# Shared expert's weights fetched early and used whole in float32 in the second mixture's first blocks

## Chip, cores and metric

One NeuronCore of a Trainium2 chip runs the whole kernel. The metric is the time of one execution in device microseconds, the median of three runs.

## What is computed

Two transformer blocks in a row on 1024 tokens of width 1024. Each is a mixer and a mixture of experts. The change lies at the seam inside the second block, between its mixer's last product and its mixture:

```python
mix = hybrid_mixer(h, ...)                      # ends with mix @ w_out
h = layer_norm(DEEPNORM_ALPHA * h + mix, ln1_g, ln1_b)
scores = jax.nn.sigmoid((xt @ w_router).astype(jnp.float32))
# top 4 of 8 groups, top 8 of 64 experts, tokens sorted by expert
yb = lax.map(block_ffn, (xin, blk_e))           # (silu(x @ w_gate[e]) * (x @ w_up[e])) @ w_down[e]
routed = jax.ops.segment_sum(y_assign, stok, num_segments=T)
shared = (jax.nn.silu(xt @ ws_gate) * (xt @ ws_up)) @ ws_down
h = layer_norm(DEEPNORM_ALPHA * h + routed + shared, ln2_g, ln2_b)
```

All inputs are float32. `ws_gate` and `ws_up` are 1024 x 256, `ws_down` is 256 x 1024: 3 MB, as each of the 64 routed experts.

## The kernel before

The program is written out by hand in the order in which each engine runs it. `mixer_out2` (line 2367) ends the second mixer: it loads `w_out` in eight pieces of 512 KB into staging places named `wo` (pool `pr`, six of them), splits every piece into a high and a low float32r part (`split`, line 240: a copy on ScalarE, a subtraction on VectorE), and then goes over the token tiles t of 128 rows: the product by `w_out` (L271 to L273, three float32r products in place of one float32 product), the layer norm (`norm`), the transposes and the router's logits of tile t - 2 (L2431, L2438). The normed rows go to `h2_d` in DRAM, scaled ones to the sum `acc_d`. The routing of tiles 0 to 3 is done in the middle (`route2`), that of tiles 4 to 7 later (`route_late`).

`moe2` (line 2569) makes a list of blocks: five token tiles for the shared expert (blocks 0 to 4), the 64 routed experts in some 100 blocks of up to 128 gathered rows (block 5 is the first), and the last three token tiles for the shared expert again. `experts` (line 1389) runs them. A block is: its rows into `xg` (`gather`), eight transposes (`trans`, L1584), the products by gate and up (`gate_up`), silu (`act`), two transposes (`h_trans`, L1643), the product by down (`down`), and an indirect DMA on GpSimd's queue that adds the result to `acc_d` (L1696).

Weights come in thirds of 1 MB (`wthird`: gate and up of half the rows twice, then down), each into one of `RAW2` = 11 places `raw` that are used in turn; third j waits until third j - 11 is freed. `pump` issues on SP's queue, in order, whatever has room; before the experts' order is known (`route` yields `ids`) it may issue only the first three thirds, those of the shared expert. An expert whose `whole` is true uses its places in float32 as they are (L1480); of another, `wsplit` writes float32r parts, in six pieces, into `gh`, `gl`, `dh`, `dl`, and the products are three float32r products each (L271 to L273). In the first blocks GpSimd makes some of the low parts (`LOD`). Routed experts that fit into 128 rows are whole, the others and the shared one are split.

While the shared blocks run, the table `ROUTE` says after which step of which block the next piece of the routing is issued: the rest of `route2`, then `rank` (the count of tokens for each expert, L2526, and the order of the experts, `ids`), the turned masks (L2551, L2559), and the tables of rows (`onehot`, `tabmm`, L1499, L1509), from which the first gathers of routed rows come. The five shared token tiles are loaded on SP's queue (L1572): tiles 0 to 3 right behind the shared weights, tile 4 after the routed thirds that `pump` has issued by then.

At the end `Last` takes places of the same ring (`room`) for the rows of `acc_d` and for the second norm's vectors.

Of the kernel before, what the change touches and what calls it, by code (L numbers as in the profile page):

```python
# [7 lines left out]
F32 = mybir.dt.float32  # L8
# [223 lines left out]
class Body:  # L232
# [1156 lines left out]
    def experts(self, cx, blocks, xsrc, wsrc, acc_d, C, route, pre=None, fin=None, whole=lambda key: False):  # L1389
# [4 lines left out]
        nc, tc = self.nc, self.tc  # L1394
        wp = cx.enter_context(tc.tile_pool(reuse_waits="tile", name="mw", bufs=2))
# [4 lines left out]
        n0 = next(n for n, b in enumerate(blocks) if b[0] is not None)  # L1400
# [10 lines left out]

        RAW = self.RAW1 if pre else self.RAW2
        raw, src, freed, ready, gone = dict(pre or {}), {}, [0], [not n0], set()
# [8 lines left out]
        def place(j):  # L1422
            if pre and j % RAW < 4:
                return self.big.tile([128, 2048], F32, name=f"b{3 - j % RAW}")
            return wp.tile([128, 2048], F32, name="raw", bufs=RAW - 4 if pre else RAW)

        def room():
            return wp.tile([128, 2048], F32, name="raw", bufs=RAW)

# [136 lines left out]
        def gather(n):  # L1566
            if n >= N:
                return
            r, t, _, R = blocks[n]
            xg = ep.tile([128, D], F32, name="xg", bufs=3)  # L1570
            if r is None:
                nc.sync.dma_start(xg, xsrc[t * 128:t * 128 + 128])  # L1572
            else:
                nc.gpsimd.indirect_dma_start(out=xg[:R], out_offset=None, in_=xsrc,
                                             in_offset=bass.IndirectOffsetOnAxis(ap=idx[n][0], axis=0))
            XG[n] = xg
# [134 lines left out]
        route = route(p1, ep)  # L1711
# [55 lines left out]
        for i, key in enumerate(keys[1:], 1):  # L1767
# [3 lines left out]
            if n0 and i > 2 and len(w) > 2:  # L1771
                w = w[1:]
# [189 lines left out]
    LOD = (0, 2, 5), (0, 3, 5)  # L1962
    LOD0 = (5,), (1, 3)

    def wthird(self, w, src, q):
# [402 lines left out]
    def mixer_out2(self, mo):  # L2368
# [5 lines left out]
        with ExitStack() as cx:  # L2374

            wr = cx.enter_context(tc.tile_pool(reuse_waits="tile", name="pr", bufs=1))
            wp = cx.enter_context(tc.tile_pool(reuse_waits="tile", name="pw", bufs=1))
# [8 lines left out]
            for n in range(4):  # L2386
                h = wp.tile([128, KT, 256], F32R, name="woh", bufs=4)
                lo = wp.tile([128, KT, 256], F32R, name="wol", bufs=4)
                for q in range(2):
                    w = wr.tile([128, 4, 256], F32, name="wo", bufs=6)  # L2390
                    nc.sync.dma_start(w, IN["w_out_2"][0][q * 512:q * 512 + 512, n * 256:n * 256 + 256]
                                      .rearrange("(k p) n -> p k n", p=128))
                    self.split(w, h[:, q * 4:q * 4 + 4], lo[:, q * 4:q * 4 + 4])
                W.append((h, lo))
# [39 lines left out]
            def router(t):  # L2434
# [8 lines left out]
                if t == 3:  # L2443
                    for _ in self.route2(rtp, lg[0], bias, 0, 4):
                        pass
            self.route_late = lambda rp: self.route2(rp, lg[1], bias, 4, 8)

            loadx(0)
            loadx(1)
            for t in range(10):  # L2450
                ts_ = slice(t * 128, t * 128 + 128)
                for half in range(2):
# [124 lines left out]
    def moe2(self, rt):  # L2577
# [28 lines left out]
        with ExitStack() as cx:  # L2606
            tp = cx.enter_context(tc.tile_pool(reuse_waits="tile", name="rt4", bufs=1))

            def route(p1, ep):
# [18 lines left out]
                for r in order:  # L2628
                    yield r
                    if r == "mask" and "pos" not in R:  # L2630
# [5 lines left out]
            fin = Last(self, cx, 8 - self.NT)  # L2636
            self.experts(cx, blocks, self.h2_d, wsrc, acc_d, C, route, fin=fin,
                         whole=lambda key: isinstance(key, int) and cap[key] <= C)

# [24 lines left out]
    def run(self):  # L2664
        tc, nc = self.tc, self.nc
        with ExitStack() as ctx:
# [49 lines left out]
            if "mxh" in self.dbg:  # L2716
                nc.sync.dma_start(self.dbg["mxh"].rearrange("k p s -> p k s"), self.mgh.bitcast(F32))
                nc.sync.dma_start(self.dbg["mxl"].rearrange("k p s -> p k s"), self.mgl.bitcast(F32))
            rp = rt.enter_context(tc.tile_pool(reuse_waits="tile", name="rt2", bufs=1))
            self.mixer_out2(rp)  # L2720
            u2.close()
# [32 lines left out]
```

## Time and profile before

| | |
|---|---|
| runs | 3248.46, 3254.14, 3257.79 us; median 3254.14 |
| profiled execution | 3251.11 us, its span 3249.3 us |
| PE, busy | 2940.6 us (90%) |
| VectorE, ScalarE, GpSimd busy | 1883.4 (58%), 1303.0 (40%), 924.9 us (28%) |
| mean granted TensorE clock | 0.952 |
| bytes read and written | 470.22 and 106.64 MB, 178 GB/s over the span |

`mixer_out2` runs from about 1981 to 2138 us, the five shared blocks from 2136 to 2256, the routed ones to about 3180, and the second norm to the end. PE stands for TensorE, DVE for VectorE, ACT for ScalarE, POOL for GpSimd, SP for the queue of SyncE that issues most DMAs. Times in rows are us from the span's start. A row of the timeline gives start, duration, engine, line, operation, tiles, shapes and count, and in brackets the idle time just before it and what ended it. The granted clock is a share of 2.4 GHz: 0.50 is the lower of the two levels, 1.2 GHz.

### The profile page before, as it was taken

Reading aid. Unit: us, or ns where it says so; the run is one execution under the profiler, and the core shown is the slowest. Engines: PE = TensorE matmul, PEld = TensorE weight load, DVE = VectorE, ACT = ScalarE, POOL = GpSimd, SP = SyncE. Lnnn points to the kernel's source line nnn. Section 1 sums busy time; section 2 is a strip of 40 time slices with the busy share of each in tenths; the row PEclk is TensorE's granted clock in tenths of the full one; section 3 lists DMA queues with packets and bytes.
Section 4 is the critical chain, followed back from the end, with each engine's and each line's share of the span. In section 5 each row is a group of like instructions: output and inputs, shape, how many; then the busy total and the mean of one; then the engine's idle time right before and its main releaser. Section 6 shows DMA issues by size and latency. Waiting matters only on the chain. (4 is left out here: it accounts for less than half of the span.)

```text
span 3249.3 us, 42976 instructions
## 1 busy us (share of the span) xinstructions
PE 2940.6 (90%) x16117; PEld 2229.6 (69%) x16117; DVE 1883.4 (58%) x2968; ACT 1303.0 (40%) x2000; POOL 924.9 (28%) x675
## 2 busy tenths in 40 slices
PE   5999999998988996999789998856999999999994
PEld 4778778886777894555479878845666666666553
DVE  5554651667777745655455566544655555555556
ACT  3332331445665423444343333332444444444442
POOL 0000000135777412333211132121333332323223
PEclk9999999998999997999899998968999999999997
DMA  3112120343223367999710003336989999999994
GB/s 113 65 52 85 65 88 7 121 158 93 86 89 92 102 240 251 309 336 350 245 53 27 27 17 101 107 116 224 289 273 320 323 317 314 313 310 317 315 287 140
DMA packets 225893, 579.79 MB, mean 178 GB/s; under 512 B 22421, under 2 KB 104005, under 8 KB 225653
## 3 DMA queue, kind: packets, MB, share of 16 engines
q1 hardware_dynamic: 188240, 445.42, 39.1%
q0 software_dynamic: 37008, 131.50, 16.3%
q8 instruction: 129, 2.11, 0.3%
q14 instruction: 84, 0.69, 0.1%
q10 hardware_dynamic: 432, 0.06, 0.0%
HBM read 470.22 MB, written 106.64 MB: 178 GB/s over the span
## 5 line engine op out<-in xcount | busy, mean ns | idle before, releaser
L1480 PE MATMUL gups<-raw,x 128*128 128x512 f32 (+1 forms) x680 | 299.2, 592 | 0.0
L271 PE MATMUL mm<-uh,wh 128*128 128x512 f32 x640 | 253.8, 396 | 10.8 <-ACT t L505 8.8
L273 PE MATMUL mm<-uh,wl 128*128 128x512 f32 x640 | 252.4, 394 | 0.0
L272 PE MATMUL mm<-ul,wh 128*128 128x512 f32 x640 | 251.7, 393 | 0.0
L1696 POOL DMA_INDIRECT acc_d<-y,si x68 | 119.8, 1761 | 413.4 <-DVE y L1693 192.6
L253 DVE TENSOR_TENSOR gl<-raw,gh 128x1024 fp32r<-128x1024 f32 x176 | 208.2, 1220 | 29.4 <-ACT gh L247 29.2
L253 POOL TENSOR_TENSOR pl<-raw,ph 128x1024 fp32r<-128x1024 f32 (+7 forms) x128 | 203.5, 1609 | 71.2 <-ACT ph L247 36.0
L1480 PEld LDWEIGHTS gups<-raw,x 128*128 128x128 f32 (+1 forms) x680 | 122.3, 185 | 146.5 <-issue 146.3
L1627 ACT ACTIVATE th<-gups 128x128 f32<-128x128 f32 (+2 forms) x136 | 49.0, 360 | 423.1 <-PE gups L1480 218.1
L272 PE MATMUL gups<-gl,xh 128*128 128x512 f32 (+1 forms) x480 | 192.8, 402 | 11.6 <-DVE gl L253 11.6
L271 PE MATMUL gups<-gh,xh 128*128 128x512 f32 (+1 forms) x480 | 198.7, 414 | 1.3 <-ACT xh L1594 0.9
L273 PE MATMUL gups<-gh,xl 128*128 128x512 f32 (+1 forms) x480 | 192.7, 401 | 0.0
L1628 DVE SCALAR_TENSOR_TENSOR hh<-th,gups 128x128 f32<-128x128 f32 (+2 forms) x136 | 53.0, 390 | 233.4 <-ACT th L1627 233.3
L247 ACT ACTIVATE gh<-raw 128x1024 fp32r<-128x1024 f32 x178 | 178.8, 1055 | 15.0 <-PE gups L273 12.7
L1693 DVE TENSOR_SCALAR y<-yps,wsl 128x512 f32<-128x512 f32 (+1 forms) x95 | 71.2, 750 | 195.7 <-ACT y L1691 191.2
L1584 PEld LDWEIGHTS tp<-ident,xg 128*128 128x128 f32 (+2 forms) x1088 | 113.6, 143 | 101.7 <-issue 44.4
L1691 ACT ACTIVATE y<-yps,wsl 128x512 f32<-128x512 f32 (+1 forms) x100 | 68.7, 687 | 275.4 <-PE yps L1480 146.9
L1584 PE MATMUL tp<-ident,xg 128*128 128x128 f32 (+2 forms) x1088 | 128.7, 262 | 42.8 <-DMA xg<-h_d 28.0
L1480 PE MATMUL yps<-raw,hT 128*128 128x512 f32 (+1 forms) x352 | 158.2, 592 | 1.4 <-ACT hT L1646 1.4
L271 PEld LDWEIGHTS mm<-uh,wh 128*128 128x128 f32 x640 | 122.2, 191 | 37.9 <-ACT t L505 10.6
L272 PEld LDWEIGHTS mm<-ul,wh 128*128 128x128 f32 x640 | 122.3, 191 | 25.6
L273 PEld LDWEIGHTS mm<-uh,wl 128*128 128x128 f32 x640 | 121.6, 190 | 26.0
(685 smaller groups left out, 7848.4 us busy)
## 6 DMA issues: line engine op xcount, KB each, us to landing
raw<-in_w_down_dram SPq DMA_DIRECT2D x86, 1024.0 KB, 8.7
raw<-in_w_gate_dram SPq DMA_DIRECT2D x170, 512.0 KB, 9.1
raw<-in_w_up_dram SPq DMA_DIRECT2D x170, 512.0 KB, 9.5
w<-in_w_in_dram SPq DMA_DIRECT2D x20, 1024.0 KB, 5.4
b<-in_w_gate_dram SPq DMA_DIRECT2D x22, 512.0 KB, 12.6
b<-in_w_up_dram SPq DMA_DIRECT2D x22, 512.0 KB, 15.1
b<-in_w_down_dram SPq DMA_DIRECT2D x10, 1024.0 KB, 16.2
w<-in_w_in_dram SPq DMA_DIRECT2D x20, 512.0 KB, 5.0
```

Source lines behind the costliest of these rows:

```text
L247: nc.scalar.activation(hi, src, AF.Copy)
L253: e.tensor_tensor(lo, src, hi.bitcast(F32), op=OP.subtract)
L271: nc.tensor.matmul(out, lh, rh, start=start and i == 0, stop=False, **kw)
L272: nc.tensor.matmul(out, lh, rl, start=False, stop=False, **kw)
L273: nc.tensor.matmul(out, ll, rh, start=False, stop=stop and i == n - 1, **kw)
L1480: nc.tensor.matmul(out, x, w, start=start and i == 0, stop=stop and i == len(pairs) - 1, **kw)
L1584: nc.tensor.transpose(ps[:, k // 4, (k % 4) * R:(k % 4) * R + R], xg[:R, k * 128:k * 128 + 128], self.ident[:R, :R])
L1627: nc.scalar.activation(th[:R, :W], ps[:R, 0:W], AF.Tanh, scale=0.5)
L1628: nc.vector.scalar_tensor_tensor(hh[:R, :W], th[:R, :W], 1.0, ps[:R, 0:W], op0=OP.add, op1=OP.mult)
L1691: nc.scalar.activation(y[:R, 0:512], ps[0][:R], AF.Copy, scale=w)
L1693: nc.vector.tensor_scalar(y[:R, 512:1024], ps[1][:R], w, None, op0=OP.mult)
L1696: nc.gpsimd.indirect_dma_start(out=acc_d, out_offset=bass.IndirectOffsetOnAxis(ap=si, axis=0), in_=y[:R], in_offset=None, compute_op=OP.add)
```

## The change

1. `mixer_out2` stages `w_out` in three places of 1 MB, `s0` to `s2` of a new pool `sh`, in place of six of 512 KB. The pool lives until the end of the mixture. Column group n goes to place n % 3, so the last one takes the first one's place.
2. Three of the eleven places of the weights' ring are those of `sh` (`shared_place`); eight stay in the pool `raw`. The shared expert's three thirds are fetched into them in `mixer_out2`, one at the start of each of the token steps t = 1, 2, 3, and handed to `experts` as `pre`.
3. The shared expert is `whole` in blocks 0 to 4: no split, float32 products. Its places are freed by the products of block 4, where they were freed by the split before. "shared again" (the last three tiles) stays split.
4. Token tiles 3 and 4 are loaded on GpSimd's queue instead of SP's.

The diff, cut to its core:

```diff
-        RAW = self.RAW1 if pre else self.RAW2
+        RAW = self.RAW2 if n0 else self.RAW1
...
         def place(j):
-            if pre and j % RAW < 4:
+            if n0 and j % RAW < 3:
+                return self.shared_place(j % RAW)
+            if not n0 and j % RAW < 4:
                 return self.big.tile([128, 2048], F32, name=f"b{3 - j % RAW}")
-            return wp.tile([128, 2048], F32, name="raw", bufs=RAW - 4 if pre else RAW)
+            return wp.tile([128, 2048], F32, name="raw", bufs=RAW - (3 if n0 else 4))
 
         def room():
-            return wp.tile([128, 2048], F32, name="raw", bufs=RAW)
+            return wp.tile([128, 2048], F32, name="raw", bufs=RAW - 3)
...
             if r is None:
-                nc.sync.dma_start(xg, xsrc[t * 128:t * 128 + 128])
+                (nc.gpsimd if 2 < n < n0 else nc.sync).dma_start(xg, xsrc[t * 128:t * 128 + 128])
...
+    def shared_place(self, j):
+        return self.sh.tile([128, 2048], F32, name=f"s{(j + 1) % 3}")
...
+                ws = self.sh.tile([128, 2048], F32, name=f"s{n % 3}").rearrange("p (q k n) -> p q k n", q=2, k=4)
                 for q in range(2):
-                    w = wr.tile([128, 4, 256], F32, name="wo", bufs=6)
+                    w = ws[:, q]
...
             for t in range(10):
+                if 0 < t < 4:
+                    self.pre2[t - 1] = self.shared_place(t - 1)
+                    self.wthird(self.pre2[t - 1], self.wsrc("_2")("shared"), t - 1)
...
-            self.experts(cx, blocks, self.h2_d, wsrc, acc_d, C, route, fin=fin,
-                         whole=lambda key: isinstance(key, int) and cap[key] <= C)
+            self.experts(cx, blocks, self.h2_d, wsrc, acc_d, C, route, self.pre2, fin,
+                         whole=lambda key: key == "shared" or isinstance(key, int) and cap[key] <= C)
```

On SP's queue, from the last steps of `mixer_out2` to the first routed thirds (`ids` is the register load that the order of the experts ends). Before, `raw` of `in_ws_gate` and its like are the shared thirds:

```order
L2404 DMA xr<-h_d 128x1024
L2442 DMA acc_d<-ah 128x1024
L1970 DMA raw<-in_ws_gate_dram 128x1024
L1971 DMA raw<-in_ws_up_dram 128x1024
L1970 DMA raw<-in_ws_gate_dram 128x1024
L1971 DMA raw<-in_ws_up_dram 128x1024
L1973 DMA raw<-in_ws_down_dram 128x2x1024
L1572 DMA xg<-h_d 128x1024 x4
L2603 TENSOR_LOAD ids_17153
```

and now, where `xr` and `acc_d` are those of the same step:

```order
L2408 DMA xr<-h_d 128x1024
L2446 DMA acc_d<-ah 128x1024
L1574 DMA xg<-h_d 128x1024 x3
L2611 TENSOR_LOAD ids_17156
```

The five DMAs of the shared thirds stand some steps further up now, and no weights are left between the mixer's last rows and the token tiles; three tiles are loaded here in place of four.

On DVE, in the routing of tiles 4 to 7, before (the rows on `gl` are low parts of the shared weights, `xl` the low part of the second token tile, `ex` the mask for which the count waits):

```order
L2489 CAST xg<-xg 128x32
L253 TENSOR_TENSOR gl_17238<-raw,gh_17236 128x1024
L2492 TENSOR_TENSOR xg<-e_r,xg 128x128
L2494 TENSOR_REDUCE y<-xg 128x32
L2495 TENSOR_SCALAR y<-y 128x32
L2496 TENSOR_TENSOR xg<-xg,y 128x256
L1595 TENSOR_TENSOR xl<-tp,xh 128x1024
L2500 MAX xg<-xg 128x8
...
L2502 TENSOR_TENSOR y<-y,xg 128x256
L2504 CAST ex<-y 128x256
L253 TENSOR_TENSOR gl_17239<-raw,gh_17237 128x1024
```

and now:

```order
L2497 CAST xg<-xg 128x32
L2500 TENSOR_TENSOR xg<-e_r,xg 128x128
L2502 TENSOR_REDUCE y<-xg 128x32
L2503 TENSOR_SCALAR y<-y 128x32
L2504 TENSOR_TENSOR xg<-xg,y 128x256
L2508 MAX xg<-xg 128x8
...
L2510 TENSOR_TENSOR y<-y,xg 128x256
L2512 CAST ex<-y 128x256
L2542 COPY cs__17293<-cnt_17276 64x64
```

The low parts are gone from the chain; the routing's own instructions follow each other.

## Rows read from the trace of the kernel before

**Rows 1.** Windows: us, busy time of each engine, granted clock, DMA share, GB/s.

```profile
2136.00:2177.00 41.00, 14.96 (x60) 11.10 (x61) 19.35 (x72) 11.55 (x12) 13.09 (x10) 0.55 0.34 115
2177.00:2209.00 32.00, 25.50 (x163) 19.71 (x161) 15.87 (x33) 9.03 (x12) 1.67 (x1) 0.95 0.71 253
...
2300.00:3150.00 850.00, 846.66 (x4764) 530.59 (x4763) 488.48 (x683) 359.79 (x539) 265.90 (x178) 1.00 0.98 311
```

**Rows 2.** Waits of PE, then of SP's queue, in the routed blocks: us, times, longest.

```profile
PE tp L1584 <- DMA xg<-h_d,gi: 3.3, 4, 1.2
...
SPq L1970 <- PE yps L1480: 272.1, 31, 11.8
...
SPq L68 <- DMA acc_d<-y,si: 31.5, 1, 31.5
```

**Rows 3.** Timeline of SP's queue from the mixer's end to the first routed thirds.

```profile
2137.14 17.18 SPq L1572 DMA_DIRECT2D xg<-h_d  x4
2185.31 0.36 SPq L1970 DMA_DIRECT2D raw<-in_w_gate_dram  x1
...
2210.41 0.33 SPq L1572 DMA_DIRECT2D xg<-h_d  x1
```

**Rows 4.** Timeline of PE, mixer's end to block 2.

```profile
2117.45 0.28 PE L273 MATMUL mm<-woh,mxl 128*128 128x256 f32 x1
...
2131.99 3.68 PE L2438 MATMUL tp<-rw,xT 128*128 128x64 f32 x16 [0.62 <-ACT xT L2432]
2147.69 1.94 PE L1584 MATMUL tp<-ident,xg 128*128 128x128 f32 x8 [12.02 <-DMA xg<-h_d]
...
2175.89 0.42 PE L2526 MATMUL cnt<-ex,onesb 128*128 128x64 bf16 x8
...
2197.45 0.50 PE L271 MATMUL gups<-gh,xh 128*128 128x512 f32 x1
```

**Rows 5.** Timeline of PE, block 2 to the second routed block.

```profile
2203.12 0.40 PE L2559 MATMUL exp<-perm,et 64*128 64x64 bf16 x8
...
2224.22 1.97 PE L1584 MATMUL tp<-ident,xg 128*128 128x128 f32 x8 [15.96 <-DMA xg<-h_d]
...
2234.21 0.39 PE L271 MATMUL yps<-dh,hTh 128*128 128x512 f32 x1
...
2236.94 0.38 PE L1643 MATMUL hT<-ident,hh 128*128 128x128 f32 x2
...
2250.00 1.09 PE L1584 MATMUL tp<-ident,xg 128*128 128x128 f32 x8 [2.23 <-DMA xg<-h_d,gi]
...
2256.15 7.03 PE L1480 MATMUL gups<-raw,x 128*128 128x512 f32 x16
...
2275.31 3.59 PE L1480 MATMUL yps<-raw,hT 128*128 128x512 f32 x8
```

**Rows 6.** Timeline of DVE: the first routing half, then the second.

```profile
2081.29 0.29 DVE L2475 TENSOR_SCALAR sc<-sc 128x256 f32<-128x256 f32 x1 [5.14 <-ACT sc L2474]
...
2090.10 0.29 DVE L2504 CAST ex<-mr 128x256 bf16<-128x256 f32 x1
...
2152.45 0.29 DVE L2475 TENSOR_SCALAR xg<-xg 128x256 f32<-128x256 f32 x1 [0.51 <-ACT xg L2474]
...
2169.49 0.29 DVE L2504 CAST ex<-y 128x256 bf16<-128x256 f32 x1
```

**Rows 7.** Timeline of ACT in block 0.

```profile
2135.83 2.03 ACT L2441 ACTIVATE ah<-xf 128x1024 f32<-128x1024 f32 x1
2149.66 1.02 ACT L1594 ACTIVATE xh<-tp 128x1024 fp32r<-128x1024 f32 x1 [11.81 <-PE tp L1584]
2150.70 1.28 ACT L2474 ACT_TABLE_LOAD   x1
```

**Rows 8.** Landing of the mixer's token rows; float32 products of the first mixture (ns min/median/max).

```profile
DMA to landing us min/median/max: 2.9/4.9/9.1
...
L1480 PE MATMUL gups<-b,x x64: 591/592/1061, 1254.2 to 1447.7; 128*96 128x512 f32 x64
```

More of the change, by code (lines that the diff above doesn't have):

```diff
@@ L2374, in mixer_out2 @@
         with ExitStack() as cx:
-            wr = cx.enter_context(tc.tile_pool(reuse_waits="tile", name="pr", bufs=1))
             wp = cx.enter_context(tc.tile_pool(reuse_waits="tile", name="pw", bufs=1))
@@ L2446, in mixer_out2 @@
             self.route_late = lambda rp: self.route2(rp, lg[1], bias, 4, 8)
+            self.pre2 = {}
             loadx(0)
@@ L2719, in run @@
             rp = rt.enter_context(tc.tile_pool(reuse_waits="tile", name="rt2", bufs=1))
+            self.sh = rt.enter_context(tc.tile_pool(reuse_waits="tile", name="sh", bufs=1))
             self.mixer_out2(rp)
```

## Prediction

> **What bounds the kernel now.** I read the windows first, to see where PE is short of work, then who waits for whom in the routed blocks, and then the timelines of SP's queue, PE, DVE and ACT at the seam between the second mixer and its mixture.
>
> The routed blocks are bound by PE: from 2300 to 3150 us it is busy 846.66 of 850 us at the full clock [rows 1], and all that it waits for is 3.3 us on gathered rows, never a weight [rows 2]. SP's queue is the one that waits, 272.1 us for the down products alone, for places to come free [rows 2]. The DMA share of 0.98 there [rows 1] shows engines with work queued, not a PE kept waiting. So whatever brings the first routed block forward brings the end forward by as much, as long as its weights are there.
>
> The five shared blocks are another thing: in the 41 us from 2136 PE has 14.96 us of work, at a mean clock of 0.55 [rows 1]. Two stalls are long. The first transposes of a token tile start at 2147.69 after 12.02 us of idling on `xg` [rows 4], because the four token tiles stand behind the shared thirds on SP's queue and issue only from 2137.14 [rows 3]. Those of tile 4 start at 2224.22 after 15.96 us [rows 5], because their load, issued at 2210.41, stands behind the routed thirds that go out from 2185.31 on [rows 3]. Between them the count of tokens, which the order of experts needs, comes at 2175.89 [rows 4]: splits and routing share DVE, whose part of the routing takes from 2152.45 to 2169.78, where the first half of the tiles took from 2081.29 to 2090.39 for the same instructions alone [rows 6].
>
> **The change, part by part,** against the profiled execution's 3251.11 us, which is 3.0 us under the median of the three runs.
>
> 1. *First token tile.* On SP only small writes are ahead of it now, and its place was the mixer's input, read until 2117.45 [rows 4]. A load of such rows lands in 2.9 to 9.1 us [rows 8], so by 2127. The router's last products end at 2131.99 + 3.68 = 2135.7 [rows 4]; the transposes follow at once instead of at 2147.69: **-12.0 us**. Bounds: 0, if something still holds the queue, and -12.0.
>
> 2. *First transposes to the count*, 28.2 us before (2147.69 to 2175.89). Now two chains run side by side. ACT ends `ah` at 2137.86, copies the transposed tile in 1.02 (no low part, no DVE), loads its table, and DVE starts 1.75 after that load's start [rows 6, 7], at 2140.6; 9.1 us of routing [rows 6] give the mask at 2149.7. PE makes the second tile's transposes (1.94) when the copy is done, until 2141, then the whole gate and up of block 0: 16 instructions, 7.03 us at the full clock [rows 5]. At the lower clock one takes 1061 ns where 592 is usual [rows 8], so 7.03 becomes 12.6. With the first third of them cold I take 9.4: 2150.4. The count follows, 14.7 us after the first transposes: **-13.5**. Bounds: -13.9 with a warm clock (DVE is then the last), -10.3 with a cold one. GpSimd's copy of the column table may slow a DVE instruction meanwhile; the cold bound covers that.
>
> 3. *Count to the end of block 1's down products.* A whole block is dearer for PE than a split one: gate and up 7.03 against 24 products from 2197.45 to 2203.12 with nothing between, 5.67; down 3.59 against 2234.21 to 2236.94, 2.73 [rows 4, 5]. That is 1.4 and 0.9. Two of each are here: +4.6, less 1.2 for the low part of a token tile that DVE no longer makes ahead of the slot numbers (two such waits of PE end there): **+3.4**. Bounds: +4.6, and +2 if the clock is warmer than before.
>
> 4. *Token tile 4.* GpSimd issues it when the third tile's transposes have freed its place, about 2152. The first routed third needs `ids`, which came 8.4 us after the count, first DMA at 2185.31, 9.4 after it [rows 3, 4]; less the low parts that DVE made between, some 2158. The tile has landed before the thirds crowd in: **-16.0**. Bounds: -16.0 and 0. I take the first because nothing is queued between 2152 and 2158.
>
>    Beside it stands a rule of the Trainium skill, "DMA: Bandwidth & Descriptors", section "Issuing engines are not separate DMA queues": transfers started by different engines run on the same 16 DMA engines and interleave, so another issuing engine saves only the time of the issue. By it this part is worth nothing, and the whole comes to 3230. No row here has a plain load on GpSimd's queue against queued weights.
>
> 5. *Tile 4 to the first routed block*, 2224.22 to 2256.15. Two gate-ups and two downs dearer: +4.6; the third down lies beside the 2.23 us in which PE waits for the gathered rows [rows 5]. Against that, before, the stall had cooled the clock: transposes of 1.97 against 1.09 [rows 5], and the products behind them; no stall, no such loss: -2.5. **+2**, bounds 0 and +6 (all at the dearer price, down of block 4 cold after the gather's wait).
>
> 6. *Cover for the weights.* Eight routed thirds go out first instead of eleven, since three places stay with the shared expert until block 4's products. Three thirds at 311 GB/s [rows 1] are 10 us. Their cover: they are third 11 to 13, the down part of the third expert and the next one's gate and up, used more than 20 us into the routed blocks, and the places free 10 us ahead of those: **0**, bounds 0 and +10.
>
> 7. *At nothing:* the fetch of the shared thirds at t = 1 to 3 (PE is busy all through, the queue's next row load is two steps early); `w_out` in three places (the same megabytes in flight; at most one piece waits for one split more, 0 to +3); the end, where the loads of the sums wait 31.5 us for the last scatter [rows 2], later than any place of the ring.
>
> Sum: -12.0 - 13.5 + 3.4 - 16.0 + 2 = **-36.1**, so 3215 us, the first routed block's gate and up at about 2220 instead of 2256.
>
> **The rivals.**
>
> *A. Tile 4 still lands behind weights* (part 4 is 0). For it: the queue's owner does not make transfers faster, and a GpSimd DMA has to be built by a busy engine. Against: its issue comes before the thirds'. 3231 us; 10%.
>
> *B. The routed thirds come short* (part 6 at +10). For it: the ring opens three places later, and the share of 0.98 leaves little to catch up with. Against: PE never waits for a weight later on. 3225 us; 7%.
>
> *C. The other side: TensorE stays at 1.2 GHz through the shared blocks.* The float32 products are then paid at 1061 instead of 592 ns. 24 instructions of a block cost 0.47 us more each, 11.3 us a block, 56 us for five, of which 2.4 are in part 2: 3215 + 54 = 3269 us. For it: 0.55 is granted in the first 41 us [rows 1]. Against: 0.95 in blocks 1 and 2, where the products are fewer and shorter than now. It decides when more than three of the five blocks run cold throughout; 5%.
>
> *D. It does not bring the head forward.* The second half of the routing could be what everything waits for, and the first tile could be held by something that the rows of before hide behind the shared thirds. Then parts 1 and 2 are nothing, and what is left is +3.4 - 16.0 + 2 = -10.6: 3240.5 us, at the edge of what can be told. Against: that half of the routing begins with ACT, which waited 11.81 us for the transposes just before it [rows 7]; 5%.
>
> **How the numbers follow.** The forecast has 73%, A 10, B 7, C 5, D 5. 3215 is the likeliest case's time. Its bounds, with parts 2, 3 and 5 at their ends, are 3211 to 3224; A and B go to 3231, so 3206 to 3233 holds the forecast, both and a spread of runs of some 4 us, and leaves out C and D and a little on either side. About 0.3%, 10 us, is what a measurement tells from no change: faster 0.92 (forecast, A, B, two in five of D), slower 0.05 (C), same 0.03 (the rest of D).
>
> **What would show it.** Transposes of `xg` right behind the router's last products at 2136 without a wait on DMA; the count at 2150 (part 2); the first routed third at 2158; no wait over 2 us at tile 4's transposes; 16 float32 instructions in 7 us for each of blocks 1 to 4; the first routed gate and up at 2220; after it no PE wait for `raw`. Wrong would be: a wait of 10 us or more on `xg` at about 2186 (A), on `raw` after 2220 (B), a clock under 0.8 from 2156 to 2216 (C), a count later than 2165 (D). If the first routed block comes at 2220 and the end does not follow, the reading of the routed blocks as bound by PE is wrong.

## The result, and the profile after

The changed kernel takes 3218.98 us (median of five runs, 3215.20 to 3221.05) where the kernel before takes 3254.14 (five runs, 3248.46 to 3257.79): a ratio of 0.989, with a 95% interval of 0.9876 to 0.9904. The predicted time was 3215, its range 3206 to 3233. The profiled execution has a span of 3217.1 us, 32.2 under that of before.

Windows of the changed kernel (columns as in [rows 1]); the first three stretches are the shared blocks' old place, the last lies in the routed blocks:

```profile
2136.00:2177.00 41.00, 36.18 (x166) 19.04 (x165) 18.98 (x94) 12.12 (x16) 5.55 (x9) 0.90 0.63 215
2177.00:2209.00 32.00, 28.05 (x118) 13.56 (x114) 14.35 (x23) 6.02 (x11) 7.97 (x6) 1.00 0.60 182
2209.00:2256.00 47.00, 42.14 (x200) 27.72 (x201) 28.70 (x54) 18.35 (x24) 9.20 (x8) 0.86 0.77 243
...
2300.00:3130.00 830.00, 826.70 (x4596) 513.52 (x4595) 468.79 (x655) 350.77 (x526) 249.84 (x174) 1.00 0.98 311
```

In the 41 us from 2136 PE has 36.18 us of work where it had 14.96, at a granted clock of 0.90 instead of 0.55 [rows 1]. The routed blocks are bound by PE as before. Its timeline from the router's last products to the routed blocks, beside [rows 4, 5]:

```profile
2131.27 3.68 PE L2442 MATMUL tp<-rw,xT 128*128 128x64 f32 x16 [0.56 <-ACT xT L2436]
2134.74 1.91 PE L1586 MATMUL tp<-ident,xg 128*128 128x128 f32 x8
...
2139.82 9.09 PE L1482 MATMUL gups<-s,x 128*128 128x512 f32 x16
2148.74 0.45 PE L2534 MATMUL cnt<-ex,onesb 128*128 128x64 bf16 x8
...
2182.50 1.04 PE L1586 MATMUL tp<-ident,xg 128*128 128x128 f32 x8
...
2210.58 1.97 PE L1586 MATMUL tp<-ident,xg 128*128 128x128 f32 x8 [4.36 <-DMA xg<-h_d,gi]
2212.34 5.23 PE L1482 MATMUL yps<-s,hT 128*128 128x512 f32 x8
2217.41 1.04 PE L1586 MATMUL tp<-ident,xg 128*128 128x128 f32 x8
2218.28 7.03 PE L1482 MATMUL gups<-raw,x 128*128 128x512 f32 x16
...
2230.07 0.59 PE L1359 MATMUL cntps<-Mb,onesb 128*128 128x64 bf16 x8 [2.93 <-DVE tb L1520]
```

Both waits on plain `xg` are gone. The count comes at 2148.74 (2175.89 before), tile 4 is turned at 2182.50 (2224.22), the first routed gate and up starts at 2218.28 (2256.15). One wait has grown, that on the first gathered rows, 4.36 for 2.23, and behind it transposes and down products take 1.97 and 5.23 us at a mean granted clock of 0.63 (2210.5 to 2217.5). "Cold" below means products at the lower level of the clock, "warm" at the upper.

SP's queue and then GpSimd's, where [rows 3] had the token tiles from 2137.14 and tile 4 at 2210.41:

```profile
2116.93 20.08 SPq L1574 DMA_DIRECT2D xg<-h_d  x3
2156.72 0.36 SPq L1975 DMA_DIRECT2D raw<-in_w_gate_dram  x1
```

```profile
2150.85 0.58 POOL L1574 DMA_DIRECT2D xg<-h_d  x1 [7.98 <-PE tp L1586]
```

Tile 4 goes out 5.9 us ahead of the first routed third and lands in 3.9 us, so it is there before that third is issued. DVE's half of the routing now runs without a split between its instructions, from 2139.76 to 2148.85, 9.1 us as in the undisturbed half of [rows 6]:

```profile
2139.76 0.29 DVE L2483 TENSOR_SCALAR xg<-xg 128x256 f32<-128x256 f32 x1 [11.14 <-ACT xg L2482]
...
2148.56 0.29 DVE L2512 CAST ex<-y 128x256 bf16<-128x256 f32 x1
```

Waits of PE from 2220 to 3130, beside [rows 2]: no wait for a weight, as before.

```profile
PE tp L1586 <- DMA xg<-h_d,gi: 3.3, 7, 1.0
PE cntps L1359 <- DVE tb L1520: 2.9, 1, 2.9
...
```

### The profile page after: what moved, and what is told of

Its sections match the earlier page's. It is cut to its first block, busy times and chain, and to the rows that moved or that the text cites. A ratio compares the mean times of both kernels' runs of the same rounds, so it can differ in the third digit from the quotient of the medians.

```text
span 3217.1 us, 42797 instructions
## 1 busy us (share of the span) xinstructions
PE 2946.9 (92%) x16057; PEld 2215.8 (69%) x16057; DVE 1867.7 (58%) x2956; ACT 1297.3 (40%) x1994; POOL 908.4 (28%) x673
## 4 chain that ended last, share of the span: by engine, by line
PE 39%; DVE 4%; DMA 4%; ACT 2%; issue 1%; POOL 1%; POOLq 0%; DVEq 0%; SPq 0%; ACTq 0%
PE gups L1482 8%; PE yps L1482 4%; PE gups L1492 3%; PE tp L1586 2%; PE gups L273 2%; PE gups L272 2%; PE gups L271 2%; PE mm L2248 2%; PE mm L2250 2%; PE mm L2249 2%; PE yps L1492 2%; DMA acc_d<-y,si 1%; PE lev L2155 1%; PE yps L271 1%; DMA xg<-h_d,gi 1%
## 5 line engine op out<-in xcount | busy, mean ns | idle before, releaser
L272 PE MATMUL mm<-ul,wh 128*128 128x512 f32 x640 | 251.5, 393 | 0.0
L273 PE MATMUL mm<-uh,wl 128*128 128x512 f32 x640 | 251.2, 393 | 0.0
L1482 PE MATMUL gups<-raw,x 128*128 128x512 f32 (+1 forms) x536 | 236.4, 592 | 0.0
L253 POOL TENSOR_TENSOR pl<-raw,ph 128x1024 fp32r<-128x1024 f32 (+7 forms) x128 | 203.6, 1610 | 73.6 <-DVE ph L251 34.7
L253 DVE TENSOR_TENSOR gl<-raw,gh 128x1024 fp32r<-128x1024 f32 x142 | 168.2, 1221 | 28.7 <-ACT gh L247 24.9
L271 PE MATMUL gups<-gh,xh 128*128 128x512 f32 (+1 forms) x440 | 179.8, 409 | 0.9 <-ACT xh L1596 0.9
L273 PE MATMUL gups<-gh,xl 128*128 128x512 f32 (+1 forms) x440 | 176.7, 401 | 0.0
L272 PE MATMUL gups<-gl,xh 128*128 128x512 f32 (+1 forms) x440 | 176.0, 400 | 0.0
L1482 PEld LDWEIGHTS gups<-raw,x 128*128 128x128 f32 (+1 forms) x536 | 95.3, 183 | 116.4 <-issue 116.4
L247 ACT ACTIVATE gh<-raw 128x1024 fp32r<-128x1024 f32 x142 | 143.0, 1054 | 11.2 <-PE gups L273 7.7
L1586 PE MATMUL tp<-ident,xg 128*128 128x128 f32 (+2 forms) x1088 | 128.6, 262 | 16.2 <-DMA xg<-h_d,gi 7.7
L273 PEld LDWEIGHTS mm<-uh,wl 128*128 128x128 f32 x640 | 121.7, 190 | 25.9
L272 PEld LDWEIGHTS mm<-ul,wh 128*128 128x128 f32 x640 | 121.8, 190 | 25.2
L1698 POOL DMA_INDIRECT h_d<-y,si x32 | 67.1, 2098 | 224.7 <-DVE y L1695 136.5
## 6 DMA issues: line engine op xcount, KB each, us to landing
b<-in_w_gate_dram SPq DMA_DIRECT2D x22, 512.0 KB, 12.5
```

The costliest lines, as they stand in the source:

```text
L247: nc.scalar.activation(hi, src, AF.Copy)
L253: e.tensor_tensor(lo, src, hi.bitcast(F32), op=OP.subtract)
L271: nc.tensor.matmul(out, lh, rh, start=start and i == 0, stop=False, **kw)
L272: nc.tensor.matmul(out, lh, rl, start=False, stop=False, **kw)
L273: nc.tensor.matmul(out, ll, rh, start=False, stop=stop and i == n - 1, **kw)
L1482: nc.tensor.matmul(out, x, w, start=start and i == 0, stop=stop and i == len(pairs) - 1, **kw)
```

## The experiments

The variants of the changed kernel have medians of four or five runs between 3217.18 and 3224.59 us, and each one's runs spread over 3 to 13 us, so a step of a few us is read from the stages of PE's timeline, which come from one profile each. The table gives, from the profiles, the time from the start of the router's last products to the first token tile's transposes, from there to the count, to tile 4's transposes, to the first routed gate and up, the sum of the four, and from there to the span's end; then the ratio to the runs of before taken beside it.

| kernel | transposes | count | tile 4 | routed | sum | to the end | ratio (95%) |
|---|---|---|---|---|---|---|---|
| before | 15.7 | 28.2 | 48.3 | 31.9 | 124.2 | 993.2 | 1 |
| changed | 3.5 | 14.0 | 33.8 | 35.8 | 87.0 | 998.8 | 0.9890 (0.9876 to 0.9904) |
| changed, again | 3.5 | 12.5 | 37.9 | 34.6 | 88.4 | 1000.8 | 0.9881 (0.9863 to 0.9899) |
| old_tile4_pool | 15.9 | 28.2 | 32.3 | 27.4 | 103.8 | 1002.2 | 0.9947 (0.9929 to 0.9964) |
| new_tiles_sp | 3.5 | 13.8 | 37.0 | 35.8 | 90.0 | 1000.5 | 0.9891 (0.9861 to 0.9921) |
| new_late_fetch | 3.5 | 13.9 | 35.5 | 34.7 | 87.7 | 1000.2 | 0.9897 (0.9862 to 0.9931) |
| new_shared_split | 3.5 | 26.3 | 32.3 | 27.3 | 89.4 | 990.1 | 0.9885 (0.9853 to 0.9916) |
| the same, again | 3.5 | 26.6 | 32.4 | 27.2 | 89.6 | 991.2 | 0.9890 (0.9873 to 0.9908) |
| new_xl_place | 3.5 | 13.8 | 35.6 | 34.7 | 87.6 | 998.2 | 0.9885 (0.9861 to 0.9909) |
| new_pad128 | 3.5 | 14.0 | 33.8 | 35.6 | 86.9 | 997.5 | 0.9897 (0.9876 to 0.9917) |
| new_tables_early | 3.5 | 11.1 | 41.7 | 32.5 | 88.8 | 1003.0 | 0.9874 (0.9850 to 0.9898) |
| new_both | 3.5 | 14.0 | 33.8 | 32.6 | 83.8 | 993.8 | 0.9884 (0.9860 to 0.9908) |
| new_split_from_2 | 3.5 | 13.8 | 35.5 | 33.7 | 86.5 | 1000.4 | 0.9879 (0.9857 to 0.9900) |
| new_best | 3.5 | 13.9 | 35.5 | 32.6 | 85.6 | 998.5 | 0.9887 (0.9866 to 0.9908) |

The same kernel's sum differs by 1.4 us between two profiles. Most of what varies is block 1's gate and up: 7.13 us in the first profile of the changed kernel (granted clock 1.00), 9.05 in the second (0.78), 8.83 in new_tiles_sp and new_late_fetch. In the second profile and in new_tables_early the count does half of its products and then waits 1.4 and 4.9 us for the mask; that wait lies in their column "tile 4".

The time to the end varies more, and without any change: before and old_tile4_pool run the same routed blocks and have 993.2 and 1002.2, of which 6.5 are PE's waits on gathered rows (3.3 and 9.8 us in all). A difference of some 9 us in that column alone shows nothing.

### Part 4 alone, on the old kernel

```diff
-                nc.sync.dma_start(xg, xsrc[t * 128:t * 128 + 128])
+                (nc.gpsimd if 3 < n < n0 else nc.sync).dma_start(xg, xsrc[t * 128:t * 128 + 128])
```

> The kernel before with one line changed: token tile 4 loaded on GpSimd's queue, nothing else of the change. Theory (part 4: the load stood behind routed thirds in SP's order): GpSimd issues it at about 2166, after its copy of the column table, ahead of the first routed third at 2185; the wait of 15.96 us before tile 4's transposes is gone, first routed gate and up at about 2240 instead of 2256, time 16 us under before (-12 to -17). Rival (the issuing engine does not matter, the 16 DMA engines are shared): the wait stays and the time is that of before, within 2 us.

3239.06 us. The wait is gone, tile 4 is turned 16.05 us earlier after the count, and the stage behind it is 4.5 us shorter too, at a granted clock of 1.00 where it was 0.85 behind the stall: 20.4 us less at the first routed block. The medians keep 17 of it (ratio 0.9947); the profiled execution, the longest of its eight, is only 6.5 under that of before, since its time to the end is 9 us longer. GpSimd's timeline, then SP's:

```profile
2183.06 0.58 POOL L1572 DMA_DIRECT2D xg<-h_d  x1 [12.22 <-PE tp L1584]
```

```profile
2190.39 0.36 SPq L1970 DMA_DIRECT2D raw<-in_w_gate_dram  x1
```

The issue comes at 2183.06, not at 2166 as I had it: what releases it are the third tile's transposes, from 2181.66 here. It is still 7.3 us ahead of the weights, and that decides. The rival falls: one line, and nothing moved but the load's place in the order.

### Part 4 undone, on the changed kernel

```diff
-                (nc.gpsimd if 2 < n < n0 else nc.sync).dma_start(xg, xsrc[t * 128:t * 128 + 128])
+                nc.sync.dma_start(xg, xsrc[t * 128:t * 128 + 128])
```

> The changed kernel with token tiles 3 and 4 back on SP's queue. Theory: tile 4's load then issues at about 2171 behind eight routed thirds, 8.4 MB, which take from 2157 until 2185 to 2192 at 250 to 300 GB/s; PE asks for it at 2182.5, so a wait of 3 to 9 us stands before its transposes and the time is 3 to 9 us above the changed kernel (not 16, since eight thirds stand ahead now where eleven stood). Rival (the issuing engine does not matter): no wait there, 0. Other rival (part 4 was worth the whole 16 here too): a wait of 14 us or more.

3221.70 us. The sum is 3.0 us longer, at the lower end of what was expected, and more than half of that is block 1's colder gate and up. SP's timeline and PE's:

```profile
2170.59 0.33 SPq L1574 DMA_DIRECT2D xg<-h_d  x1
```

```profile
2184.49 1.09 PE L1586 MATMUL tp<-ident,xg 128*128 128x128 f32 x8 [0.93 <-DMA xg<-h_d]
```

So one and the same line is worth 20 us on the old kernel and 1 to 3 on the new. In the old one eleven thirds stand ahead of the load, and SP waits among them, 12.7 us in all, for earlier weights to land; the longest of these waits, from 2180 to 2225 in the kernel before:

```profile
SPq L1970 <- DMA raw<-in_w_down_dram: 4.6, 2, 2.6
SPq L1971 <- DMA raw<-in_w_up_dram: 2.6, 2, 1.9
...
```

So the load goes out 25.1 us after the first third, at 2210.41 [rows 3]. In new_tiles_sp eight thirds stand ahead, with 5.2 us of such waits, and it goes out after 14.7. It takes about 14 us to land in both, and PE now asks for it 27.7 us after the first third where it asked after 23.0. The 10.4 us that it goes out sooner and the 4.7 that it is asked for later are the 15 us that this stall is shorter: it lands just when PE wants it.

### The fetch put back to its old time

```diff
-                if 0 < t < 4:
-                    self.pre2[t - 1] = self.shared_place(t - 1)
-                    self.wthird(self.pre2[t - 1], self.wsrc("_2")("shared"), t - 1)
```

> The changed kernel without the fetch in the token steps 1 to 3: the shared thirds are issued where the old kernel issued them, after the mixer's last rows on SP, but into the three places that the change made and used whole. Theory: what held the token tiles in the old kernel was the place of the last shared third, which could be written only when the mixer's last rows had been read; with places that are free by then the thirds go out at about 2106 and land by 2120, the first token tile still lands by 2130, first transposes at 2135, time as the changed kernel, -2 to +3 us. Rival (the order on SP is what counts, so the early fetch is what brought part 1): first transposes at 2140 to 2147, 5 to 12 us above the changed kernel.

```profile
2109.34 0.49 SPq L1975 DMA_DIRECT2D s<-in_ws_gate_dram  x1
...
2112.39 0.44 SPq L1978 DMA_DIRECT2D s<-in_ws_down_dram  x1
2120.21 20.07 SPq L1574 DMA_DIRECT2D xg<-h_d  x3
```

The first transposes follow the start of the router's last products by 3.47 us, as in the changed kernel. SP issues all the shared thirds by 2112.8; in old_tile4_pool, with the old places, the second third went out 29 us after the first, at 2140.65, and what SP waited for last was PE's reading of the mixer's rows in the router's last products:

```profile
SPq L1970 <- PE tp L2438: 6.3, 1, 6.3
```

What part 1 gained comes from the free places. The median is 3224.59, 5.6 us above the changed kernel's where -2 to +3 was expected, but from runs of 3216.29 to 3228.75 (ratio 0.9897 for 0.9890): a gain by the early fetch is seen neither there nor in the stages.

### The shared expert split, everything else as changed

```diff
-                         whole=lambda key: key == "shared" or isinstance(key, int) and cap[key] <= C)
+                         whole=lambda key: isinstance(key, int) and cap[key] <= C)
```

> The changed kernel with the shared expert split again, as in the old kernel (early fetch, places and GpSimd's queue as changed). Theory (the splits share DVE with the second half of the routing): transposes at 2135 as in the changed kernel, but the count at about 2164 instead of 2149; five blocks cheaper for PE by some 2.3 us each give back 7 or 8, so 3 to 12 us above the changed kernel. Rival (early weights alone are enough, and using them whole only costs PE): the count at about 2150, and 5 to 11 us below the changed kernel.

The count comes 26.3 us after the first transposes: 12.3 of part 2's 14.2 us are gone, as the theory has it. DVE's timeline shows what stands between the routing's instructions:

```profile
2143.56 1.21 DVE L253 TENSOR_TENSOR gl<-s,gh 128x1024 fp32r<-128x1024 f32 x1
2144.70 2.45 DVE L2500 TENSOR_TENSOR xg<-e_r,xg 128x128 f32<-128x128 f32 x1
...
2147.51 1.92 DVE L2503 TENSOR_SCALAR y<-y 128x32 f32<-128x32 f32 x1
```

A mask product of 0.29 us usually (2144.82 in the changed kernel) takes 2.45 while GpSimd makes low parts, a small scalar product 1.92 for 0.18. Yet the whole is not 10 us slower: after the count the split blocks win 9.9 us back (59.7 us from the count to the first routed block against 69.5), because their products are cheaper and the wait for the gathered rows is 1.9 instead of 4.4. At the first routed block the whole weights are 1 to 2.6 us ahead. Behind it they take 8 to 11 us longer (990 and 991 us to the end against 999 and 1001); some 3 of these the next two kernels explain, the rest lies within what the column varies without a change. In the medians the two are not told apart, here (3217.19 us) or a second time:

> The changed kernel with the shared expert split, a second time, beside the changed kernel. Theory (whole weights bring the first routed block forward by 2 to 3 us and cost the routed blocks 6 us by the place of xl and hTl): router to first routed block 89 to 90 us, products at 390 to 393 ns, 3 to 4 us below the changed kernel. Rival (whole weights are worth some 10 us as the sum of parts 2, 3 and 5 has it): 8 us or more above the changed kernel.

3220.99 us beside 3218.79 of the changed kernel; the theory's 3 to 4 us below is not seen in the medians, the rival's 8 above neither.

> The changed kernel as it is, a second time, beside the other kernels of this call: 3215 to 3222 us by all theories; it tells how far stages of one and the same kernel differ from run to run (the router's last products to the first routed block: 87 us in the first run; from there to the end 999 us).

3218.79 us, as expected; the spread of the stages is the one given above.

### Where the low parts lie

The three profiles with split shared weights have 390 to 393 ns for the float32r products on L272 and L273 in the routed blocks, the three with whole ones 395 to 397, from kernels that do the same there.

```diff
+                if n == 0 < n0:
+                    ep.tile([128, 8, C], F32R, name="xl")
```

> The changed kernel with one tile moved: the pool gives places in the order in which tiles are first asked for, and since no shared block makes low parts any more, the low part xl of the token tile is asked for last and lies 19328 bytes higher. Here it is asked for once at block 0, so that it gets the old kernel's place back; nothing else of the work changes. Theory (the place of xl costs the routed blocks some 5 ns for each float32r product: mean 395 to 397 ns in the three kernels with whole shared weights, 390 to 391 in the three with split ones): products back at 390 to 391 ns, some 1,200 of them, 5 to 6 us below the changed kernel. Rival (another chip, another hour, or the place of another tile): 395 to 397 ns stay and so does the time.

Groups of the changed kernel, then of new_xl_place, from 2300 to 3100 (busy us, mean ns):

```profile
L273 PE MATMUL gups<-gh,xl 128*128 128x512 f32 x227 | 90.0, 397 | 0.0
L272 PE MATMUL gups<-gl,xh 128*128 128x512 f32 x227 | 89.8, 395 | 0.0
...
L273 PE MATMUL yps<-dh,hTl 128*128 128x512 f32 x112 | 44.3, 395 | 0.0
L272 PE MATMUL yps<-dl,hTh 128*128 128x512 f32 x112 | 44.2, 395 | 0.0
```

```profile
L273 PE MATMUL gups<-gh,xl 128*128 128x512 f32 x224 | 87.5, 391 | 0.0
L272 PE MATMUL gups<-gl,xh 128*128 128x512 f32 x224 | 87.3, 390 | 0.0
L273 PE MATMUL yps<-dh,hTl 128*128 128x512 f32 x112 | 44.3, 395 | 0.0
L272 PE MATMUL yps<-dl,hTh 128*128 128x512 f32 x112 | 44.2, 395 | 0.0
```

Gate and up are back at 390 and 391 ns; down, whose `hTl` was not moved, stays at 395. So it is the tile's place. Is it how high, or where it begins?

```diff
+            if n == n0 + 1 and n0:
+                ep.tile([128, 32], F32, name="pad", bufs=1)
```

> The changed kernel with 128 unused bytes in each partition ahead of the place of xl: xl goes from byte 218912 to 219040 of a partition and hTl from 227104 to 227232, still at the top of the memory; nothing else differs. In all runs so far the low parts with 390 to 393 ns a product begin 416 bytes above a multiple of 512, as xh and hTh do, and those with 395 to 397 ns 288 bytes above one. Theory (where the low part begins within some hundred bytes counts, not how high it lies): 390 to 391 ns for gate and up, 390 to 393 for down, 6 us less PE work in the routed blocks. Rival (how high it lies counts): 395 to 397 ns stay.

```profile
L273 PE MATMUL gups<-gh,xl 128*128 128x512 f32 x224 | 87.5, 391 | 0.0
L272 PE MATMUL gups<-gl,xh 128*128 128x512 f32 x224 | 87.3, 390 | 0.0
...
L273 PE MATMUL yps<-dh,hTl 128*128 128x512 f32 x112 | 44.0, 393 | 0.0
L272 PE MATMUL yps<-dl,hTh 128*128 128x512 f32 x112 | 43.7, 390 | 0.0
```

128 unused bytes put both right, with the tiles still at the top and no other tile moved: it is where they begin. The whole shared weights had moved `xl` and `hTl` behind small tables whose sizes are not round. What it is worth I had put too high, at 6 us, since these products overlap: from the first to the last product, a split block's gate and up takes 5.40 us in the changed kernel and 5.33 in new_pad128, its down 2.65 and 2.63. That is 0.09 us a block, some 3 us over 35 blocks. In the medians it does not show (3220.36 us in new_xl_place, 3223.08 in new_pad128).

### The routing's tables one block earlier

```diff
-            if n == n0 - 1:
+            if n == n0 - 2:

                 gate_up(n, lambda: (tabmm(n0, n0), tabmm(n0 + 1, n0), onehot(n0 + 2)))
...
-            if n0 and n == n0 - 2:
+            if n0 and n == n0 - 3:
                 onehot(n0)
```

> The changed kernel with the tables of the first three routed blocks made one block earlier (one-hot rows at the end of block 2, their products inside block 3's gate and up). Theory: the first gather then issues at about 2193 instead of 2203 and its rows are there before PE asks at 2206; the wait of 4.36 us goes, and so do the cold transposes and down products behind it (1.97 and 5.23 us against 1.04 and 3.60), less some 1 us for products that wait on the one-hot rows in block 3: 5 to 7 us below the changed kernel, first routed gate and up 80 to 82 us after the router's last products start instead of 87. Rival (the gathered rows come late because the routed thirds fill the DMA engines, not because of the issue): the wait stays at 3 us or more, 0 to 2 us gained.

> Both of the two edits together: the old place of xl and the tables one block earlier. They act in different stretches, so the theory expects the sum, 10 to 13 us below the changed kernel, about 3207 us. Rival for either: what is missing from the sum is the one that is wrong.

The wait on gathered rows falls from 4.4 to 1.6 us in both kernels, and a new one of 1.4 on DVE's half of the down product's result takes a part. In new_both the sum is 83.8, 3 to 5 us under the changed kernel's. The medians, 3217.60 and 3217.18 us, show neither the 5 to 7 us nor the 10 to 13 that were expected below the changed kernel. In new_tables_early the sum is 88.8, for another reason: the clock was at its upper level already in block 0 (granted 1.00 from 2136 to 2144), whose gate and up took 7.03 us, and PE then waited for the mask and cooled (0.67 from 2149 to 2163). Its waits up to the first routed block:

```profile
PE cnt L2534 <- DVE ex L2512: 4.9, 1, 4.9
...
PE tp L1586 <- DMA xg<-h_d,gi: 1.6, 1, 1.6
```

PE's timeline there:

```profile
2136.76 7.03 PE L1482 MATMUL gups<-s,x 128*128 128x512 f32 x16
...
2148.76 0.37 PE L2534 MATMUL cnt<-ex,onesb 128*128 128x64 bf16 x4 [4.85 <-DVE ex L2512]
2149.07 0.59 PE L2536 MATMUL cnt<-onesb,ex 128*64 128x1 bf16 x8
2149.58 1.97 PE L1586 MATMUL tp<-ident,xg 128*128 128x128 f32 x8
```

The transposes behind the wait take 1.97 us, 1.09 in the changed kernel, and block 1's gate and up 9.09. Not all of the wait comes from the warm block 0. The mask itself is 2.1 us late here, 16.2 us after the first transposes instead of 14.1: the first instruction of DVE's routing takes 2.39 us where it takes 0.29 [rows 6], beside GpSimd's copy of the column table, against which part 2 of the prediction warned. GpSimd reaches that copy sooner because it follows the second tile's transposes, which are warm too.

```profile
2137.53 2.39 DVE L2483 TENSOR_SCALAR xg<-xg 128x256 f32<-128x256 f32 x1 [11.12 <-ACT xg L2482]
```

```profile
2137.86 1.91 POOL L2541 COPY cols<-tilep 128x1536 bf16<-128x1536 bf16 x1
```

With the mask at its usual time a warm block 0, through 11.1 us after the first transposes, would still wait 3 us for it: the mask sets the count.

### Whole weights for two blocks only

This is new_both with one thing more: the six split pieces are issued at the end of block 0, and blocks 2 to 4 use them.

```diff
+        wh = lambda n: whole(blocks[n][2]) and not 2 <= n < n0
...
+            for _ in range({0: 6}.get(n, 0) if n0 else 0):
+                piece(0)
```

> Both edits, and the shared weights used whole in blocks 0 and 1 only; their six split pieces go on ACT, DVE and GpSimd at the end of block 0, after the count and the order of experts, and blocks 2 to 4 use float32r parts. Theory (the whole weights pay only where they take the splits off the routing's path; each later block is 2.3 us cheaper split): 7 us less of PE's work, of which 2 to 3 go to waits on low parts that DVE makes: 3 to 6 us below the kernel with both edits. Rival (the chain of the routing's tables, not PE, sets the first gather, and the splits slow it on DVE): no gain or 1 to 4 us lost.

Sum 86.5 against 83.8, median 3217.39 us against 3217.18: the gain is not there, and the rival fits. How much is lost is not shown, since 1.7 of the 2.7 us are a colder gate and up in block 1. PE waits 2.9 us for one-hot rows and 2.1 for the gathered rows; two low parts took DVE 5.41 us beside GpSimd's, before the mask of the slots.

GpSimd, busy with its own low parts, issues tile 4 only at 2166.86, among the routed weights, which go out on SP from 2160.18. The landing of the 1 MB that SP issues at 2166.72, then that of the tile's 512 KB:

```profile
DMA to landing us min/median/max: 17.3/17.3/17.3
```

```profile
DMA to landing us min/median/max: 7.5/7.5/7.5
```

### All that looked useful together

The tables early, both low parts at their old places, and the change shown:

```diff
...
-             (1, 3): 1, (2, 1): 1, (2, 2): 1, (5, 3): 1}
+             (1, 3): 1, (2, 1): 1, (2, 2): 1, (6, 0): 1}
```

> The tables one block earlier, both low parts (xl and hTl) at their old places, and the second piece of the slot work (the products on L1359 that wait 2.93 us for DVE in every run) issued after block 6's gate and up instead of before it. Theory: against the changed kernel's profile 3 us less from the router to the first routed block (84 instead of 87), 3 us for the wait on L1359 and 2 to 3 us for the cold products behind it, 6 us for the products: 13 to 15 us, 3202 to 3206 us where the changed kernel has 3217 to 3219. Rival (the wait at L1359 only moves to the products behind it): 9 to 11 us.

```profile
PE tp L1586 <- DMA xg<-h_d,gi: 8.9, 5, 3.3
```

The wait on L1359 is gone from the routed blocks, but the next piece behind it, the gathered rows of block 8, then waits 3.32 us, and the rows waited for come to 8.9 us in this run (1.0 to 9.8 over all profiles). The median is 3219.75 us (ratio 0.9887) beside 3218.79 (0.9881) of the changed kernel: both the 13 to 15 us of the theory and the 9 to 11 of the rival failed. The stages up to the first routed block gained 1.4 to 2.8 of the 3 us hoped for there; the rest does not arrive. No version here is faster than the changed kernel by what the medians can tell.

## Why the prediction was right

The time fell in the range, 4 us from its likeliest value, 3 of them because the sum started from a profiled execution 3 us under the median: the medians differ by 35.2 where the sum says 36.1. The mechanisms in front of the routed blocks came out as worked out. That the sum came so close is in part luck: steps 3 and 5 missed by 2.0 and 1.9 us in opposite directions. What the working left out is a loss behind these steps, of which the runs show some 4 us.

1. *First token tile, -12.0.* From the router's last products to the first transposes 15.7 became 3.5: **-12.2**, with no wait on DMA. The step rested on the queue before the tile; new_late_fetch shows that the last shared thirds' places, not the time of the fetch, had held that queue.
2. *To the count, -13.5, bounds -13.9 to -10.3.* **-14.2**, just past the warm end. Gate and up took 9.09 us, five of its sixteen products cold. I took 9.4 for a cold third, though my prices, 12.6 and 7.03, give 8.9; and 12.6 came from the duration of one product, where what counts is how they follow each other, every 0.85 us cold and 0.43 warm here. The mask came at 2148.85, just when PE was through with them: the two chains were as even as the working had them. new_shared_split gives 12.3 of it back, so the splits on DVE were the cause.
3. *Count to the end of block 1, +3.4, bounds +2 to +4.6.* Tile 4's transposes follow the end of block 1's down products at once, 33.8 us after the count; before it was 32.4 to the same point (48.3 less the stall): **+1.4**. The mechanism was right and the term too large by 2, below its bounds: the old blocks had run partly cold (granted clock 0.85 in the 11 us from the count, 1.00 now; transposes of masks 1.06 us, 0.63 now), which I had only let into the lower bound.
4. *Tile 4, -16.0.* **-16.0**: turned without a wait, issued at 2150.85 (2152 predicted), ahead of a first third at 2156.72 (2158). old_tile4_pool measures 17 us for the line alone: what the load had waited for was its turn on SP's queue, and from GpSimd's it goes out ahead of the weights, 7.3 us there and 5.9 here. One run has the two together: in new_split_from_2 GpSimd issues tile 4 6.7 us after the first third, and it lands in 7.5 us, where 1 MB of weights that SP issues 0.14 us earlier takes 17.3 and tile 4 behind weights on SP's own queue some 14. By the Trainium skill, "DMA: Bandwidth & Descriptors", section "Issuing engines are not separate DMA queues", this part would be worth nothing. That transfers of several engines interleave, as the Trainium skill says there, agrees with these landings; that only the time of the issue is saved does not agree with the 16 us. The step did not see that three weights fewer ahead of the load would have taken most of the stall away without GpSimd: undone, the part costs 3.0 us at most, so the 16 us at which rival A is priced were not at stake in this kernel.
5. *Tile 4 to the first routed block, +2, bounds 0 to +6.* **+3.9**. I had counted block 4's down products beside an unchanged wait of 2.23 us; the wait became 4.36, since PE now comes to the gathered rows sooner than the tables do (a block earlier for the tables makes it 1.6), and 1.97 and 5.23 us were paid cold behind it.
6. *Cover for the weights, 0.* **0**: no wait for `raw` or `s` in the routed blocks.

Together -37.1 from the router's last products to the first routed gate and up (124.2 to 87.0) for -36.1. Behind that point the working had nothing, and the profile has **+5.7** (993.2 to 998.8). Two parts of it are the change's: 1.25 us because more products run cold behind the wait on L1359 (eleven at 0.63 us from 2231.04, six before), and some 3 us for the place of the low parts. The rest, in the rows' arrival and the end, is less than what old_tile4_pool and before differ by in the same work. Part 7, the work held at nothing, comes to -0.7 in the mixer, which shows nothing: the router's last products start anywhere from 2129.0 to 2138.2 us in the profiles of the changed kernel and its variants. So 32.2 of 36.1 us arrived in the profile; the medians differ by 35.2, within what two sets of runs can differ.

The rivals: A and B fall by the waits, C by the clock (0.90 and 1.00 in the first two windows), D by the first two stages. What the prediction never asked is which half of the change earns the time. The sum -13.5 + 3.4 + 2 reads as if the whole weights were worth 8 us. The split variant says 1 to 2.6 at the first routed block, and nothing in the medians: of the 12 us gained at the count, dearer products and a longer wait for the gathered rows take back 10.

## What to carry to other kernels

Before a load is moved to another queue, ask what stands ahead of it and what that waits for. Free places for the shared weights and a way out ahead of the routed ones were worth nearly all of this change. Tile 4's stall had two remedies, another queue or fewer weights ahead of the load; each alone took nearly all of it, so together they were worth no more than one. Work taken off one engine's path is only worth what the next chain leaves of it: 12 us at the count were 2 at the first routed block. And a tile that is no longer asked for early moves others in memory, so compare the mean duration of unchanged products before and after.

## What was not expected of the hardware

Float32r products took 390 to 393 ns or 395 to 397 in the mean according to where the low part of the stationary operand (`xl`, `hTl`) begins: 416 bytes above a multiple of 512 or 288. Moving both low parts by 128 bytes changed it back, nothing else being moved. The products on L272, whose own operands had not moved, change with those on L273 that follow them. Which step in the address decides was not tried.

In the shared blocks the granted clock rose at different times in profiles of one kernel: block 1's gate and up took 7.13 us (granted 1.00) or 9.05 (0.78) in the changed kernel, and the first routed block came 1.4 us later. What decides it was not tried.

Beside work of GpSimd on its own data, short instructions of DVE took 1.9 to 2.5 us where they take 0.2 to 0.3: in new_tables_early beside a copy, in new_shared_split beside subtractions.
